# Gate and up products of a conv FFN: from three 256-column products to one of 512 and one of 256, with each exit split over steps

## The chip, the core and the metric

The kernel runs on one core of one Trainium2 chip. Engines with queues of their own work side by side: PE (TensorE) does matrix products and, as PEld, loads their stationary operands; DVE (VectorE) and ACT (ScalarE) do elementwise work; SP issues most of the DMA loads and POOL a few. Each engine takes its instructions strictly in the order in which the program issued them, and an instruction that has to wait holds up all behind it on its engine. The metric is the device time of one execution in microseconds (us); the median of three runs of the kernel before is 438.47 us.

## What is computed

One layer of a small hybrid block over 256 tokens with 1024 channels: a token mixer (block attention and retention), a layer norm, a convolutional feed-forward part, a layer norm. The change touches the feed-forward part alone:

```python
def conv_ffn(h, w_ff_gate, w_ff_up, ff_conv_w, ff_conv_b, w_ff_down):
    s = h.shape[1]
    g = h @ w_ff_gate
    u = h @ w_ff_up
    gp = jnp.pad(g, ((0, 0), (CONV_WIDTH - 1, 0), (0, 0)))
    g_conv = sum(gp[:, j:j + s, :] * ff_conv_w[j] for j in range(CONV_WIDTH)) + ff_conv_b
    a = jax.nn.gelu(g_conv, approximate=False) * u
    return a @ w_ff_down
```

D_FF is 2816, the convolution is three tokens wide, and all is in float32.

## The kernel before

**Precision.** A float32 value is held as two tiles, high and low: high is the value copied into PE's float32r type, low is what is left. `split` (line 64) makes them: ACT copies the high part, DVE subtracts. A product of two such values is three products on PE (`mm3`, line 79): high × high (line 80), high × low (81) and low × high (82).

**Units and steps.** The weights come from memory in units of 128 × 2048 (1 MB), each used in two halves of 1024 columns. From line 230 on, the program is a list of steps; a step uses one half (or, at the two groups by `weights4`, several). The main loop (line 1055) goes through the steps in order. In step s it first runs the side work (`run_sides`, generators such as `residual`, which multiplies and adds the first norm's rows, line 966), then prepares halves ahead (`prep_to`, `prep_halves`): ACT writes `whi` (line 1009) and DVE `wlo` (line 1023), and the raw buffer that comes free is filled by the next load on SP's queue (`load_raw`, line 73, 4 buffers). At most 8 prepared halves are alive; in the FFN the kernel prepares one more in each step, whose buffers are those that the step before has given back. Then it issues the step's products and, at the end of a unit, its exit. Some weight units of the modulation vector run through the same stream and are reduced on DVE (`ada`, line 147).

**The FFN.** A unit r of 256 hidden channels has a gate product (`ffn_gate`), an up product (`ffn_up`) and a down product (`mk_down`); there are NR = 11. The tokens' hidden state after the first norm, transposed, lies in four tiles: `S["h2h"]` (high, slots 3a and 3b) and `S["h2l"]` (low, slots 6a and 6b), each 128 × 4 × 256. In `wstat8` (line 287) a gate or up half is 128 hidden channels by 256 tokens, summed over 8 k with 3 products of 256 columns each; both halves of a unit share one PSUM bank of 512 columns. Four banks (0 to 3) go round (`one_bank`).

Up units 0 and 1 are made in another form before the gates (`xs_group`, steps 52 to 55). From step 56 on the order is: gate 0, gate 1, gate 2, up 2, down 0, down 1, and then gate r, up r, down r − 1 up to r = 7; then gate and up of 8, 9 and 10; then the downs of units 7 to 10 in the order of the output (`tok0`, `tok1`), with the second norm. Each unit is two steps; gate 0 is steps 56 and 57, down 1 steps 66 and 67. Within gate 0, between its halves, PE transposes the last tokens of up 0 and 1 (`up_T`, line 577).

**The exits.** When both halves of a gate unit are done, `gate_done` (line 586) issues: ACT twice `Identity` with the convolution's middle weight and bias, out of PSUM (line 593); DVE four `scalar_tensor_tensor`, out of PSUM, for the other two taps (line 596); ACT `Gelu` (line 598). When an up unit is done, `act_in` (line 604) multiplies the up values in PSUM by the Gelu values on DVE (line 606) and splits the result into `ah` and `al` (lines 65 and 66), the stationary operands of `down` (line 615). For units 0 and 1 `act_in` follows the gate's exit at once. All of an exit is issued in one go, at the end of the unit's second step.

Of the kernel before, what the change touches and what calls it, by code (L numbers as in the profile page):

```python
# [7 lines left out]
F32 = mybir.dt.float32  # L8
# [42 lines left out]
def _body(nc, a, out, pe, act, dve, sp, cst, wts, big, tmp, ps, dram):  # L51
    f = lambda ap: ap.bitcast(F32)

    def bank(i):
        return ps.tile([128, 512], F32, tag=f"P{i}", name=f"P{i}")

    def slot(n, shape, dt=F32):
        return big.tile(shape, dt, tag=f"A{n}", name=f"A{n}")

    def halves(n):  # L60

        return [slot(n + e, [128, 4, 256], F32R) for e in "ab"]

    def split(hi, lo, src):
        act.activation(hi, src, AF.Copy)  # L65
        dve.tensor_tensor(lo, src, f(hi), OP.subtract)  # L66
# [12 lines left out]
    def mm3(o, lh, ll, rh, rl, start, stop):  # L79
        pe.matmul(o, lh, rh, start=start, stop=False)  # L80
        pe.matmul(o, lh, rl, start=False, stop=False)  # L81
        pe.matmul(o, ll, rh, start=False, stop=stop)  # L82

    def table(func):

        d_ = tmp.tile([128, 1], F32, name="dummy", bufs=1)
        act.activation(d_, epst, func)
# [13 lines left out]
    bcol = const("bcol", [128, 6, 8], nc.gpsimd)  # L101
    mod = cst.tile([128, 6, 8], F32, name="mod")

    raws = {}
    loads_A = [(dict(a="ada1", W="winA", X="winX")[n], j) for n, j in SEQ if n in "aWX"]

# [196 lines left out]
    def wstat4(name, u, xh, xl, done):  # L303
# [9 lines left out]
            return mm  # L313
        weights(a[name][u], mk(0), mk(1))

    S = {}
    ghh, ghl = (lambda k: hh[:, k]), (lambda k: hl[:, k])

# [200 lines left out]
        weights4(src, [mk(0, 0), mk(0, 1), mk(1, 0), mk(1, 1)], [range(4)] * 4)  # L519

    def out_start():
        S["h2h"], S["h2l"] = halves("3"), halves("6")
        GB = S["GB"] = tmp.tile([128, 2, 8], F32, name="GB", bufs=1)
        m = mod[:, 2:4]
        lncol = consts["lncol"]
        dve.tensor_tensor(GB[:, 0], lncol[:, 0], m[:, 0], OP.mult)
        dve.tensor_tensor(GB[:, 1], lncol[:, 1], m[:, 0], OP.mult)
        dve.tensor_tensor(GB[:, 1], GB[:, 1], m[:, 1], OP.add)
        table(AF.Sqrt)
# [46 lines left out]
    def up_T(t):  # L576
        p = bank(6 + t)
        for i in range(4):
# [4 lines left out]
             {(0, 1, "mid"): ln1_tok1, (0, 1): lambda p: up_tokens(0, p),  # L583
              (1, 1, "mid"): lambda: up_T(0), (1, 1): lambda p: (up_tokens(1, p), table(AF.Gelu))})

    def gate_done(r):
        def fn(p):
            g = slot(("5", "15")[r % 2], [128, 2, 256])
            pv = p.rearrange("p (i t) -> p i t", i=2)
            convw = consts["convw"]  # L590
            w = lambda n, i: convw[:, n, 2 * r + i:2 * r + i + 1]
            for i in range(2):
                act.activation(g[:, i], pv[:, i], AF.Identity, scale=w(2, i), bias=w(3, i))
            for n in (1, 0):
                for i in range(2):
                    dve.scalar_tensor_tensor(g[:, i, 2 - n:], pv[:, i, :254 + n], w(n, i), g[:, i, 2 - n:],
                                             op0=OP.mult, op1=OP.add)
            act.activation(g, g, AF.Gelu)
            S["gelu", r] = g
            if r < 2:  # L600
                act_in(r, S["uT"][:, 2 * r:2 * r + 2].rearrange("p a b -> p (a b)"))
        return fn

    def act_in(r, u):
        g = S.pop(("gelu", r)).rearrange("p a b -> p (a b)")
        dve.tensor_tensor(g, u, g, OP.mult)
        ah = slot(("9a", "9b", "10a", "8a")[r % 4], [128, 2, 256], F32R)
        al = slot(("2a", "2b", "4", 0)[r % 4], [128, 2, 256], F32R)
        split(ah.rearrange("p a b -> p (a b)"), al.rearrange("p a b -> p (a b)"), g)
        S["a", r] = ah, al  # L610

    def up_done(r):
        return lambda p: act_in(r, p)

    def down(r, t, hf, hl_, cs, first, last, p=None):
        ah, al = S["a", r]
# [34 lines left out]
    def tok0(i):  # L651
        def fn(ts):
            if i == 0:
                table(AF.Sqrt)
            for hf in range(2):
                down(NR - NG + i, 0, hf, ts[hf], BOTH, False, i == NG - 1 and hf == 1)
            if i == NG - 1:
                n = Norm(S["x1"][:, 0], S["g", 1], S["z2"][0], ("6a", "6b"))
                for c, w in BOTH:
                    n.piece(c, w, S["yf"][c // 512])  # L660
                S["rows"] = out_rows(n, 0, BOTH)
                next(S["rows"])
        return fn
# [23 lines left out]
                    pass  # L687
        return fn

    def ffn_gate(r):  # L690
        wstat8("wgate", r, gh2, gl2, gate_done(r))

    def ffn_up(r):
        wstat8("wup", r - 2, gh2, gl2, up_done(r))

    def first():
        bank_i[0] = 0
        up_T(1)

    wstat8("wgate", 0, gh2, gl2, gate_done(0), first)  # L700
    ffn_gate(1)
    for r in range(2, NR):
        ffn_gate(r)
# [169 lines left out]
    def retention():  # L873
        rT, decay, sms = S["rT"], S["decay"], S["sms"]
        while S["main"] < RV_AT:
            yield
            yield
            yield
        rv = S["rv"]
        yr = [slot(n, [128, 1024]) for n in ("8a", "8b")]  # L880
        stt = tmp.tile([128, 8, 6], F32, name="stt", bufs=1)
        mv = tmp.tile([128, 8, 2], F32, name="mvr", bufs=1)
        sd = tmp.tile([128, 8], F32, name="sdr", bufs=1)
        ds_ = {}
        for h in range(HR + 2):
            yield
            if h > 1:
                g = h - 2
                for t in range(2):
                    dve.bn_stats(stt[:, 2 * g + t], yr[t][:, g * 256:(g + 1) * 256])  # L890
                    dve.bn_aggr(mv[:, 2 * g + t], stt[:, 2 * g + t:2 * g + t + 1])
            yield
            if 0 < h <= HR:
                g = h - 1
                d_ = ds_.pop(g)
                p = bank(7)
                c = slice(g * 256, (g + 1) * 256)
                pe.matmul(p[:, 0:256], d_[:, 0:128], rv[0][:, c], start=True, stop=True)
                pe.matmul(p[:, 256:512], d_[:, 128:256], rv[0][:, c], start=True, stop=False)
                pe.matmul(p[:, 256:512], d_[:, 256:384], rv[1][:, c], start=False, stop=True)  # L900
                for t in range(2):
                    act.activation(yr[t][:, c], p[:, t * 256:(t + 1) * 256], AF.Copy)
            if h < HR:
                p = bank(4)
                pe.matmul(p[:, 0:256], rT[1][:, h, 0:128], rT[0][:, h, :], start=True, stop=True)
                pe.matmul(p[:, 256:384], rT[1][:, h, 128:256], rT[0][:, h, 128:256], start=True, stop=True)
                d_ = sms[:, (HM + h) % (TL + 2)]
                dve.tensor_tensor(d_, p[:, :384], decay[h // 2][:, h % 2], OP.mult)
                ds_[h] = d_
            yield  # L910
        S["x"] = [slot(n, [128, 1024]) for n in ("2a", "2b")]
        for i in range(2):
            nc.gpsimd.dma_start(S["x"][i], a["x"][i])
        yield
        act.activation(sd, mv[:, :, 1], AF.Sqrt, bias=epst)
        dve.reciprocal(sd, sd)
        yield
        yield
        while S["main"] < RG_AT:
            yield  # L920
            yield
            yield
        srg = S["rg"]
        for g in range(HR + 1):
            yield
            if g:
                for t in range(2):
                    act.activation(yr[t][:, c], yr[t][:, c], AF.Copy, scale=sd[:, 2 * g + t - 2:2 * g + t - 1])
            if g < HR:
                c = slice(g * 256, (g + 1) * 256)  # L930
                for t in range(2):
                    dve.scalar_tensor_tensor(yr[t][:, c], yr[t][:, c], mv[:, 2 * g + t, 0:1], srg[t][:, c],
                                             op0=OP.subtract, op1=OP.mult)
            yield
            yield
        yrh, yrl = halves("3"), halves("6")
        S["yrh"], S["yrl"] = yrh, yrl
        for _ in range(3):
            yield
        for w in range(2):  # L940
            for t in range(2):
                yield
                yield
                p = bank(4 + t)
                for i in range(4):
                    pe.transpose(p[:, i * 128:(i + 1) * 128],
                                 yr[t][:, w * 512 + i * 128:w * 512 + (i + 1) * 128], ident)
                pv = p.rearrange("p (i t) -> p i t", i=4)
                split(yrh[w][:, :, t * 128:(t + 1) * 128], yrl[w][:, :, t * 128:(t + 1) * 128], pv)
                yield  # L950
# [99 lines left out]
    def run_sides():  # L1050
        for g in list(sides):
            if next(g, StopIteration) is StopIteration:
                sides.remove(g)

    for s, (need, rel, fn) in enumerate(steps):
# [6 lines left out]
        if not late:  # L1062
            prep_to(max(need) + 1 + (LOOKAHEAD if s < LN1_AT - 1 else HL_BUFS))
        run_sides()
        fn([tiles[h] for h in need])
        for h in rel:
            tiles.pop(h)
# [100 lines left out]
```

## Time and profile before

| what | value |
|---|---|
| median of three runs | 438.47 us (438.03 to 438.67) |
| the profiled execution, device time | 439.22 us |
| its span, first to last instruction | 437.4 us |
| PE, DVE, ACT busy | 420.7, 345.9, 241.4 us |
| FFN in the trace | gate 0 from 253.8 us, last up ends at about 407, last product ends at about 429.9 |
| units in it | 11 gates, 9 ups, 11 downs |
| mean granted clock | 0.994 |

The page gives the busy time of each engine and its share of the span; the chain of waits follows the work that ended last back to its start. A row of the timeline has the start in us from the span's beginning, the duration, engine, line, operation, result and operands, shape and count; what stands in brackets is the idle time before it and what ended it. A row with a count over one shows several instructions in sequence as one piece. A matmul's duration includes its passage through the array, so that the distance from start to start is what it costs in a stream.

### The profile page before, as it was taken

Reading aid. Unit: us, or ns where it says so; the run is one execution under the profiler, and the core shown is the slowest. Engines: PE = TensorE matmul, PEld = TensorE weight load, DVE = VectorE, ACT = ScalarE, POOL = GpSimd, SP = SyncE. Lnnn points to the kernel's source line nnn. Section 1 sums busy time; section 2 is a strip of 40 time slices with the busy share of each in tenths; the row PEclk is TensorE's granted clock in tenths of the full one; section 3 lists DMA queues with packets and bytes.
Section 4 is the critical chain, followed back from the end, with each engine's and each line's share of the span. In section 5 each row is a group of like instructions: output and inputs, shape, how many; then the busy total and the mean of one; then the engine's idle time right before and its main releaser. Section 6 shows DMA issues by size and latency. Waiting matters only on the chain.

```text
span 437.4 us, 6902 instructions
## 1 busy us (share of the span) xinstructions
PE 420.7 (96%) x2732; PEld 379.7 (87%) x2732; DVE 345.9 (79%) x547; ACT 241.4 (55%) x368; POOL 7.3 (2%) x17
## 2 busy tenths in 40 slices
PE   2999999999999999999999999999999999999993
PEld 1878888777788999999989899899999999999882
DVE  4888689969997999698779887798896665576476
ACT  4366568579873469543443894665445445355500
POOL 0000000000000000000000010000000000000000
PEclk9999999999999999999999999999999999999997
DMA  7998997795468778789664069477766774550001
GB/s 266 397 417 338 335 339 281 291 349 211 180 239 306 285 288 303 267 289 352 222 240 145 0 232 412 166 273 272 283 227 254 290 263 171 194 192 2 1 24 72
DMA packets 19728, 105.72 MB, mean 242 GB/s; under 512 B 2528, under 2 KB 4592, under 8 KB 8432
## 3 DMA queue, kind: packets, MB, share of 16 engines
q1 hardware_dynamic: 18288, 100.27, 61.5%
q0 software_dynamic: 1408, 5.01, 3.3%
q8 instruction: 21, 0.34, 0.3%
q14 instruction: 11, 0.09, 0.0%
HBM read 104.22 MB, written 1.06 MB: 241 GB/s over the span
## 4 chain that ended last, share of the span: by engine, by line
PE 83%; DVE 9%; ACT 3%; DMA 2%; issue 1%; SPq 1%; DVEq 0%; ACTq 0%
PE P L80 25%; PE P L82 25%; PE P L81 25%; DVE junk L147 3%; DMA raw<-in_ada 2%; DVE wlo L1023 2%; ACT whi L65 1%; DVE wlo L66 1%; PE P L513 1%; PE P L516 1%; PE P L515 1%; PE P L809 1%; PE P L828 1%; PE P L852 1%; SPq L73 1%
## 5 line engine op out<-in xcount | busy, mean ns | idle before, releaser
L1023 DVE TENSOR_TENSOR wlo<-raw,whi 128x1024 fp32r<-128x1024 f32 x118 | 140.6, 1220 | 24.7 <-ACT whi L1009 24.7
L1009 ACT ACTIVATE whi<-raw 128x1024 fp32r<-128x1024 f32 x118 | 120.2, 1052 | 41.0 <-PE P L82 11.9
L82 PE MATMUL P<-whi,A 128*128 128x512 f32 (+1 forms) x228 | 87.3, 383 | 0.0
L80 PE MATMUL P<-whi,A 128*128 128x512 f32 (+1 forms) x184 | 72.9, 396 | 5.4 <-ACT A L65 5.3
L81 PE MATMUL P<-wlo,A 128*128 128x512 f32 (+1 forms) x184 | 71.0, 386 | 0.0
L147 DVE CUSTOM_DVE_ANT_0 junk<-raw,srow 128x1024 bf16<-128x1024 f32 (+1 forms) x49 | 58.8, 1200 | 1.5 <-DMA raw<-in_ada 1.1
L80 PE MATMUL P<-A3a,whi 128*128 128x256 f32 x192 | 54.4, 283 | 0.0
L82 PE MATMUL P<-A3b,wlo 128*128 128x256 f32 x192 | 54.4, 283 | 0.0
L81 PE MATMUL P<-A6a,whi 128*128 128x256 f32 x192 | 54.4, 283 | 0.0
L80 PE MATMUL P<-A3b,whi 128*128 128x256 f32 x192 | 54.4, 283 | 0.0
L81 PE MATMUL P<-A6b,whi 128*128 128x256 f32 x192 | 54.3, 283 | 0.0
L82 PE MATMUL P<-A3a,wlo 128*128 128x256 f32 x192 | 54.3, 283 | 0.0
L82 PEld LDWEIGHTS P<-whi,A 128*128 128x128 f32 x228 | 43.5, 191 | 8.8 <-DVE A L66 0.3
L80 PEld LDWEIGHTS P<-whi,A 128*128 128x128 f32 x184 | 35.3, 192 | 14.1 <-ACT A L65 6.6
L80 PE MATMUL P<-A,whi 128*128 128x256 f32 x160 | 46.0, 287 | 0.0
L81 PE MATMUL P<-A,whi 128*128 128x256 f32 x160 | 45.3, 283 | 0.0
L82 PE MATMUL P<-A,wlo 128*128 128x256 f32 x160 | 45.3, 283 | 0.0
L81 PEld LDWEIGHTS P<-wlo,A 128*128 128x128 f32 x184 | 35.2, 192 | 6.3
L80 PEld LDWEIGHTS P<-A3a,whi 128*128 128x128 f32 x192 | 36.8, 192 | 0.3
L81 PEld LDWEIGHTS P<-A6a,whi 128*128 128x128 f32 x192 | 36.8, 192 | 0.3
L81 PEld LDWEIGHTS P<-A6b,whi 128*128 128x128 f32 x192 | 36.9, 192 | 0.0
L80 PEld LDWEIGHTS P<-A3b,whi 128*128 128x128 f32 x192 | 36.9, 192 | 0.0
(227 smaller groups left out, 705.5 us busy)
## 6 DMA issues: line engine op xcount, KB each, us to landing
raw<-in_ada SPq DMA_DIRECT2D x23, 1024.0 KB, 5.7
raw<-in_wup SPq DMA_DIRECT2D x11, 1024.0 KB, 4.8
raw<-in_wgate SPq DMA_DIRECT2D x11, 1024.0 KB, 4.9
raw<-in_wdown SPq DMA_DIRECT2D x11, 1024.0 KB, 4.8
raw<-in_winB SPq DMA_DIRECT2D x10, 1024.0 KB, 6.8
raw<-in_winA SPq DMA_DIRECT2D x16, 256.0 KB, 6.9
raw<-in_winA SPq DMA_DIRECT2D x4, 1024.0 KB, 6.2
raw<-in_winGr SPq DMA_DIRECT2D x4, 1024.0 KB, 5.6
```

What stands on the lines that cost most here:

```text
L65: act.activation(hi, src, AF.Copy)
L66: dve.tensor_tensor(lo, src, f(hi), OP.subtract)
L73: sp.dma_start(t[:, i * n:(i + 1) * n], src[:, i * n:(i + 1) * n])
L80: pe.matmul(o, lh, rh, start=start, stop=False)
L81: pe.matmul(o, lh, rl, start=False, stop=False)
L82: pe.matmul(o, ll, rh, start=False, stop=stop)
L147: dve.tensor_tensor_reduce(out=junk[:, rows], in0=raw[:, rows], in1=srow[:, rows], scale=1.0, scalar=0.0, op0=OP.mult, op1=OP.add, accum_o ...
L513: pe.matmul(p, xl(k)[:, tk], hi[:, c], start=False, stop=k == 7)
L515: pe.matmul(p, xh(k)[:, tk], hi[:, c], start=k == 0, stop=False)
L516: pe.matmul(p, xh(k)[:, tk], lo[:, c], start=False, stop=False)
L1009: act.activation(hi, src, AF.Copy)
L1023: dve.tensor_tensor(lo, src, f(hi), OP.subtract)
```

## The change

The high and low parts of the hidden state are put beside each other in one tile, so that one product of 512 columns multiplies a weight tile with both; the product of the low weights with the high tokens stays 256 columns wide. Per k there are two products in place of three, with two weight loads in place of three. The bank now holds one half: columns 0 to 255 sum high × high and low × high, columns 256 to 511 high × low. Leaving the bank, ACT copies the second part into a tile, and DVE adds the first to it. Each half of a unit has a bank of its own, in a round of the same four.

The convolution's middle tap moves from ACT to DVE, and reads the tile instead of PSUM, as do the other two taps. The work of an exit is no longer issued in one go: `put_off` puts it on a list with the step at which it is due, and the main loop issues what is due after the preparation of halves and ahead of the step's products.

```diff
+    place = {"3a": ("Ya", 0), "6a": ("Ya", 1), "3b": ("Yb", 0), "6b": ("Yb", 1)}
+    pairs = {}
+
+    def reopen(dt, *names):
+        for n in names:
+            pairs[n] = big.tile([128, 2, 1024], dt, tag=f"A{n}", name=f"A{n}")
...
+    def mm2(o, wh, wl, x2, start, stop):
+        if start:
+            pe.matmul(o, wh, x2, start=True, stop=False)
+        pe.matmul(o[:, :256], wl, x2[:, 0], start=False, stop=False)
+        if not start:
+            pe.matmul(o, wh, x2, start=False, stop=stop)
...
+    def wstat8m(name, u, x2, copy, done, mid=None):
+        def mk(half):
+            def mm(hi, lo):
+                if half and mid:
+                    mid()
+                p = one_bank()
+                for k in range(8):
+                    mm2(p, hi[:, k * 128:(k + 1) * 128], lo[:, k * 128:(k + 1) * 128], x2(k), k == 0, k == 7)
+                t = copy(half)
+                act.activation(t, p[:, 256:], AF.Copy)
+
+                def rest():
+                    dve.tensor_tensor(t, p[:, :256], t, OP.add)
+                    done(half)
+                put_off(1, rest)
+            return mm
+        weights(a[name][u], mk(0), mk(1))
+
+    waiting = []
+
+    def put_off(n, fn):
+        waiting.append((S["main"] + n, fn))
...
     def out_start():
-        S["h2h"], S["h2l"] = halves("3"), halves("6")
+        S["h2"] = [slot("Y" + e, [128, 2, 4, 256], F32R) for e in "ab"]
+        S["h2h"], S["h2l"] = [[t[:, i] for t in S["h2"]] for i in range(2)]
...
     def gate_done(r):
-        def fn(p):
-            g = slot(("5", "15")[r % 2], [128, 2, 256])
-            pv = p.rearrange("p (i t) -> p i t", i=2)
+        def fn(half):
+            g, x = gu(r)[:, half], gu(r)[:, 2 + half]
             convw = consts["convw"]
-            w = lambda n, i: convw[:, n, 2 * r + i:2 * r + i + 1]
-            for i in range(2):
-                act.activation(g[:, i], pv[:, i], AF.Identity, scale=w(2, i), bias=w(3, i))
+            w = lambda n: convw[:, n, 2 * r + half:2 * r + half + 1]
+            dve.tensor_scalar(g, x, w(2), w(3), op0=OP.mult, op1=OP.add)
             for n in (1, 0):
-                for i in range(2):
-                    dve.scalar_tensor_tensor(g[:, i, 2 - n:], pv[:, i, :254 + n], w(n, i), g[:, i, 2 - n:],
-                                             op0=OP.mult, op1=OP.add)
-            act.activation(g, g, AF.Gelu)
-            S["gelu", r] = g
-            if r < 2:
-                act_in(r, S["uT"][:, 2 * r:2 * r + 2].rearrange("p a b -> p (a b)"))
+                dve.scalar_tensor_tensor(g[:, 2 - n:], x[:, :254 + n], w(n), g[:, 2 - n:],
+                                         op0=OP.mult, op1=OP.add)
+            if half:
+                put_off(min(r, 1), lambda: act.activation(gu(r)[:, :2], gu(r)[:, :2], AF.Gelu))
+                if r < 2:
+                    put_off(1 + r, lambda: act_in(r, S["uT"][:, 2 * r:2 * r + 2]))
         return fn
...
-        split(ah.rearrange("p a b -> p (a b)"), al.rearrange("p a b -> p (a b)"), g)
         S["a", r] = ah, al
+        put_off(min(r, 1), lambda: act.activation(ah, g, AF.Copy))
+        put_off(1 + min(r, 1), lambda: dve.tensor_tensor(al, g, f(ah), OP.subtract))
 
     def up_done(r):
-        return lambda p: act_in(r, p)
+        return lambda half: act_in(r, gu(r)[:, 2:]) if half else None
...
         run_sides()
+        for e in waiting:
+            if e[0] <= s:
+                e[1]()
+        waiting[:] = [e for e in waiting if e[0] > s]
         fn([tiles[h] for h in need])
```

`gu(r)` is a tile of 128 × 4 × 256 in slot 5 or 15: its first two parts hold the gate after the convolution, its last two what comes out of the banks (the gate's, then the up's). The slots 3a, 6a, 3b and 6b, which other stages use for other tiles, become views of the two paired tiles Ya and Yb; `reopen` makes these anew at three places (the start, the normalised retention output, the end).

More of the change, by code (lines that the diff above doesn't have):

```diff
@@ L55, in bank @@
         return ps.tile([128, 512], F32, tag=f"P{i}", name=f"P{i}")
-    def slot(n, shape, dt=F32):
-        return big.tile(shape, dt, tag=f"A{n}", name=f"A{n}")
+    place = {"3a": ("Ya", 0), "6a": ("Ya", 1), "3b": ("Yb", 0), "6b": ("Yb", 1)}
[3 more added lines that the diff above has]
+            pairs[n] = big.tile([128, 2, 1024], dt, tag=f"A{n}", name=f"A{n}")
+    def slot(n, shape, dt=F32):
+        if n not in place:
+            return big.tile(shape, dt, tag=f"A{n}", name=f"A{n}")
+        pair, e = place[n]
+        assert pairs[pair].dtype == dt
+        v = pairs[pair][:, e, :math.prod(shape[1:])]
+        return v.rearrange("p (a b) -> p a b", a=shape[1]) if len(shape) == 3 else v
     def halves(n):
@@ L102, in _body @@
     mod = cst.tile([128, 6, 8], F32, name="mod")
+    reopen(F32, "Ya", "Yb")
     raws = {}
@@ L584, in _body, with gu @@
               (1, 1, "mid"): lambda: up_T(0), (1, 1): lambda p: (up_tokens(1, p), table(AF.Gelu))})
+    def gu(r):
+        if ("gu", r) not in S:
+            S["gu", r] = slot(("5", "15")[r % 2], [128, 4, 256])
+        return S["gu", r]
     def gate_done(r):
-        def fn(p):
-            g = slot(("5", "15")[r % 2], [128, 2, 256])
-            pv = p.rearrange("p (i t) -> p i t", i=2)
+        def fn(half):
+            g, x = gu(r)[:, half], gu(r)[:, 2 + half]
             convw = consts["convw"]
-            w = lambda n, i: convw[:, n, 2 * r + i:2 * r + i + 1]
-            for i in range(2):
-                act.activation(g[:, i], pv[:, i], AF.Identity, scale=w(2, i), bias=w(3, i))
+            w = lambda n: convw[:, n, 2 * r + half:2 * r + half + 1]
+            dve.tensor_scalar(g, x, w(2), w(3), op0=OP.mult, op1=OP.add)
             for n in (1, 0):
-                for i in range(2):
-                    dve.scalar_tensor_tensor(g[:, i, 2 - n:], pv[:, i, :254 + n], w(n, i), g[:, i, 2 - n:],
-                                             op0=OP.mult, op1=OP.add)
-            act.activation(g, g, AF.Gelu)
-            S["gelu", r] = g
-            if r < 2:
-                act_in(r, S["uT"][:, 2 * r:2 * r + 2].rearrange("p a b -> p (a b)"))
+                dve.scalar_tensor_tensor(g[:, 2 - n:], x[:, :254 + n], w(n), g[:, 2 - n:],
[4 more added lines that the diff above has]
+                    put_off(1 + r, lambda: act_in(r, S["uT"][:, 2 * r:2 * r + 2]))
         return fn
     def act_in(r, u):
-        g = S.pop(("gelu", r)).rearrange("p a b -> p (a b)")
+        g = gu(r)[:, :2]
         dve.tensor_tensor(g, u, g, OP.mult)
@@ L657, in fn @@
             if i == NG - 1:
+                reopen(F32, "Ya", "Yb")
                 n = Norm(S["x1"][:, 0], S["g", 1], S["z2"][0], ("6a", "6b"))
@@ L688, in tok1, with ffn_gate @@
         return fn
-    def ffn_gate(r):
-        wstat8("wgate", r, gh2, gl2, gate_done(r))
+    h2 = lambda k: S["h2"][k // 4][:, :, k % 4]
+    def ffn_gate(r, mid=None):
+        wstat8m("wgate", r, h2, lambda half: gu(r)[:, 2 + half], gate_done(r), mid)
     def ffn_up(r):
-        wstat8("wup", r - 2, gh2, gl2, up_done(r))
+        wstat8m("wup", r - 2, h2, lambda half: gu(r)[:, 2 + half], up_done(r))
     def first():
-        bank_i[0] = 0
         up_T(1)
-    wstat8("wgate", 0, gh2, gl2, gate_done(0), first)
+    ffn_gate(0, first)
     ffn_gate(1)
@@ L935, in retention @@
             yield
+        reopen(F32R, "Ya", "Yb")
         yrh, yrl = halves("3"), halves("6")
```

## The prediction

> **What bounds the kernel now.** I read the page first (shares, then the chain of waits), then busy times by stretch, then the timeline of each engine in the FFN.
>
> ```profile
> span 437.4 us, 6902 instructions
> PE 420.7 (96%) x2732; PEld 379.7 (87%) x2732; DVE 345.9 (79%) x547; ACT 241.4 (55%) x368; POOL 7.3 (2%) x17
> PE 83%; DVE 9%; ACT 3%; DMA 2%; issue 1%; SPq 1%; DVEq 0%; ACTq 0%
> 257.00:280.00 23.00, 23.00 (x183) 22.53 (x182) 17.95 (x25) 14.80 (x22) 2.08 (x4) 1.00 0.85 328
> 280.00:300.00 20.00, 20.00 (x135) 18.55 (x134) 17.46 (x23) 11.43 (x14) 0.00 (x0) 1.00 0.72 257
> 300.00:320.00 20.00, 20.00 (x135) 18.52 (x134) 16.43 (x23) 9.63 (x12) 0.00 (x0) 1.00 0.66 252
> 340.00:360.00 20.00, 20.00 (x147) 19.04 (x147) 13.24 (x18) 9.53 (x12) 1.07 (x2) 1.00 0.78 289
> ```
>
> The columns after the stretch are its length and the busy time of PE, PEld, DVE, ACT and POOL. In the FFN, PE is never idle, at full clock; it sets the end. But DVE is at 87% from 280 to 300, so it has little to spare where the change gives it work.
>
> How PE spends its time is read from start to start of its products:
>
> ```profile
> 282.05 0.39 PE L80 MATMUL P<-whi,A9a 128*128 128x512 f32 x1
> ...
> 283.87 0.39 PE L82 MATMUL P<-whi,A2b 128*128 128x512 f32 x1
> ...
> 299.32 0.28 PE L80 MATMUL P<-A3b,whi 128*128 128x256 f32 x1
> 299.44 0.28 PE L81 MATMUL P<-A6b,whi 128*128 128x256 f32 x1
> 299.56 0.28 PE L82 MATMUL P<-A3b,wlo 128*128 128x256 f32 x1
> 299.68 0.40 PE L80 MATMUL P<-whi,A10a 128*128 128x512 f32 x1
> ...
> 304.93 0.39 PE L82 MATMUL P<-whi,A 128*128 128x512 f32 x1
> 305.15 0.28 PE L80 MATMUL P<-A3a,whi 128*128 128x256 f32 x1
> ```
>
> After a 256-column product the next starts 0.120 us later, whatever its width. The eight starts of 512 columns from 282.05 to 283.87 are 0.2275 us apart, less than two of 256; the one before a 256 (304.93 to 305.15) is no longer.
>
> **What PE gains.** Each k of a gate or up half now takes three products of 256 columns (0.360 us), and then one of 512 and one of 256 (0.2275 + 0.120): 0.0125 us less. There are 20 units (11 gate, 9 up) of 2 halves and 8 k: 320 × 0.0125 = 4.0 us, 0.10 us for each half. The moving operand of the new product comes in two runs of 256 columns; no row shows such an operand. Its price lies between nothing and 0.0125 us (which would make 512 columns as dear as two 256s, and the gain nil); I take nothing, since all the rows of 512, whose operands are weight tiles, are alike.
>
> The Trainium skill (TensorE: Matmul & The Clock Gate, section Back-to-back issue gap) gives a warm gap of N / 2.4 plus about 2.5 ns, so that merging two products saves only the 2.5 ns: an estimate of 320 × 2.5 ns = 0.8 us. The rows show 12.5 ns where the page has 2.5, and the measurement decides.
>
> **What the exits cost.** Before, a gate unit leaves PSUM after both halves: two L593 on ACT, four L596 on DVE, Gelu. After, each half leaves with a copy of 256 columns on ACT, then on DVE an add (out of PSUM), a tensor_scalar, and two scalar_tensor_tensor, each on the result of the one before. An up half gets a copy and an add. The rows for these, DVE first (the line of L470 is a group: count, busy us, mean ns):
>
> ```profile
> 238.22 0.67 DVE L449 TENSOR_SCALAR A<-A,mv,sd 128x768 f32<-128x768 f32 x1
> L470 DVE TENSOR_SCALAR A7b<-P,GB 128x128 f32<-128x128 f32 x8 | 2.7, 404 | 0.5 <-PE P L457 0.5
> 257.33 5.77 DVE L1023 TENSOR_TENSOR wlo<-raw,whi 128x1024 fp32r<-128x1024 f32 x5 [1.53 <-ACT whi L1009]
> 263.01 1.65 DVE L596 SCALAR_TENSOR_TENSOR A<-P,convw,A 128x255 f32<-128x255 f32 x4
> 265.42 0.69 DVE L606 TENSOR_TENSOR A<-A,A 128x512 f32<-128x512 f32 x1 [0.76 <-ACT A L598]
> 287.37 0.69 DVE L966 TENSOR_TENSOR A<-A,A 128x512 f32<-128x512 f32 x1
> 287.97 2.35 DVE L1023 TENSOR_TENSOR wlo<-raw,whi 128x1024 fp32r<-128x1024 f32 x2
> 429.92 0.42 DVE L402 TENSOR_TENSOR A6a<-P,AR 128x256 f32<-128x256 f32 x1 [0.51 <-PE P L82]
> 430.38 0.42 DVE L403 TENSOR_TENSOR A7b<-A7b,A6a 128x256 f32<-128x256 f32 x1
> 141.32 0.38 ACT L902 ACTIVATE A8a<-P 128x256 f32<-128x256 f32 x1 [3.10 <-PE P L900]
> 141.60 0.38 ACT L902 ACTIVATE A8b<-P 128x256 f32<-128x256 f32 x1
> 256.25 4.84 ACT L1009 ACTIVATE whi<-raw 128x1024 fp32r<-128x1024 f32 x5
> 264.76 0.63 ACT L598 ACTIVATE A<-A 128x512 f32<-128x512 f32 x1 [2.28 <-DVE A L596]
> 266.15 0.63 ACT L65 ACTIVATE A9a<-A 128x512 fp32r<-128x512 f32 x1 [0.76 <-DVE A L606]
> 266.69 1.99 ACT L1009 ACTIVATE whi<-raw 128x1024 fp32r<-128x1024 f32 x2
> ```
>
> A dependent step costs its duration and 0.03 (430.38 − 429.92 = 0.46 after a 0.42); an independent one starts about 0.08 before the other ends, so a wlo holds DVE 1.14 (five in 5.77) and a 512-column step 0.60 (287.97 − 287.37). A scalar_tensor_tensor is 0.48, or 0.39 with independent neighbours. The tensor_scalar isn't shown at this size: by proportion of L449 0.22, on the line through L470 (0.40 for 128) and L449 (0.67 for 768) 0.46. I take 0.41, nearer to the upper row, as the small size pays mostly a fixed part. A gate half then holds DVE 0.46 + 0.44 + 0.51 + 0.39 = 1.80 us, a unit 3.6 where it was 1.6; an up unit gets two adds, 0.8 more. The ACT copy is 0.38, holds 0.28, and is no dearer than what it replaces in a gate.
>
> **Where that lands: the first ten steps of the FFN.** Main steps 56 to 66 are gate 0, gate 1, gate 2, up 2 (two halves each), down 0 (64, 65) and the first half of down 1 (66). That half's third product reads al of unit 1, which L66 wrote well ahead before (the row is below). In the changed program al(1) is issued in step 64, and DVE works strictly in order. Ahead of it, from 257.33, stand: wlo of halves 60 to 71 (one more is issued in each step, ahead of that step's deferred work), 12 × 1.14 = 13.7; six gate halves (gates 0, 1, 2), 6 × 1.80 = 10.8; the multiplication and al of unit 0 and the multiplication of unit 1, 3 × 0.60 = 1.8; the add of the first up half, 0.35. Together 26.6. DVE also stands still where ACT's queue makes it wait: ACT holds gelu(0), behind which come a copy and whi(66), which the next wlo needs, so that after the exit of gate 0 DVE idles 0.1 + 0.55 + 0.28 + 1.05 = 2.0; behind ah(0) 0.3; behind gelu(2) 0.6. That is 257.33 + 26.6 + 2.9 = 286.8, and al(1), at 0.69, ends at 287.5.
>
> ```profile
> 273.83 0.69 DVE L66 TENSOR_TENSOR A2b<-A,A9b 128x512 fp32r<-128x512 f32 x1 [0.70 <-ACT A9b L65]
> ...
> 282.73 0.39 PE L80 MATMUL P<-whi,A9b 128*128 128x512 f32 x1
> 282.96 0.39 PE L81 MATMUL P<-wlo,A9b 128*128 128x512 f32 x1
> 283.19 0.39 PE L82 MATMUL P<-whi,A2b 128*128 128x512 f32 x1
> ```
>
> A2b is al(1): it was written by 274.5, and its reader started at 283.19. With eight halves 0.10 faster PE would be there at 282.4. It waits until 287.5: **5.1 us** of stops. Some 2 us fall earlier, because a gate or up half now takes a bank of four: up 2's halves need banks 0 and 1 back from gate 1, whose adds come out of the same DVE queue about 1 us late each. The other 3 us fall at step 66.
>
> Bounds: all six tensor_scalars at 0.22 take 1.1 off; 0.1 more on every new step adds 2.5 (24 in the gates, one add). So stops of 4.0 to 7.6, and with the 4.0 gained a net of 0 to +3.6; my value is **+1.1**.
>
> **After that** nothing else waits. A cycle of gate, up and down takes PE 16.6 us, and DVE gets 2 + 0.8 = 2.8 more in it: from 280 to 300 17.46 + 2.8 × 20 / 16.6 = 20.8 of 20, from 300 to 320 19.8, then less. A lag of 1 us is covered: wlo is prepared eight halves ahead, and a bank is asked for again five steps (14 us) after its product while downs stand between, three steps (8 us) in the last gates, where DVE (13.24 of 20 now) has room. If that cover were gone, this lag would be paid, 1 to 2 us. The loads on SP's queue follow wlo as before, 4 buffers ahead. The paired h2 tile holds the same bytes in the same order of writes, so everything ahead of step 56 costs nothing more: writers and readers stay far apart under PE's products. The tail from 418 on has the same steps; al(10) is wanted in the fourth tail step, 8 us after its copy, and needs about 4.
>
> **The clock** adds to this. What a stop of PE does to it shows only at the ends of the run:
>
> ```profile
> 10.33 0.80 PE L80 MATMUL P<-whi,A 128*128 128x512 f32 x1 [5.26 <-ACT A L65]
> 12.20 0.63 PE L81 MATMUL P<-wlo,A 128*128 128x512 f32 x1
> 12.63 0.63 PE L82 MATMUL P<-whi,A 128*128 128x512 f32 x1
> 15.61 0.40 PE L80 MATMUL P<-whi,A 128*128 128x512 f32 x1
> 431.00:432.00 1.00, 0.00 (x0) 0.00 (x0) 0.93 (x3) 0.29 (x1) 0.00 (x0) 1.00 0.00 0
> 432.00:433.00 1.00, 0.00 (x0) 0.00 (x0) 1.00 (x4) 0.00 (x0) 0.00 (x0) 0.51 0.00 0
> ```
>
> The last product ended by 429.92 (L402 above waited for it), and from 432.0 on the granted clock is one half: 2.1 us of rest were enough. At the start, after a wait of 5.26 us, products of 512 columns start 0.43 us apart (12.20, 12.63) until 15.6: the 5.3 us from 10.33 on at this pace cost 5.3 × (1 − 0.23 / 0.43) = 2.5 us. A stop of 3 us in step 66 may bring this: 0 to 2.5, and I take 0.9, since one sighting at an end says little of when the clock falls within.
>
> The Trainium skill (same page, section What's actually happening) has the clock halved after an idle window of about 3.4 us, and back after a busy one. An estimate by it: 3.4 × 0.47 = 1.6 us if the stop fills enough of a window. The trace's fall after 2.1 us of rest is earlier than a whole window.
>
> **Sum.** 437.4 − 4.0 + 5.1 + 0.9 = 439.4 us of span, +2.0. The profiled execution lasted 439.22 (1.8 around its span), 0.75 over the median 438.47; on the scale of the median, **440.5 us**.
>
> **Rivals.** (1) The stops happen, but the clock holds: +1.1, 439.6; for it, the stop is in pieces; against it, the fall after 2.1 us. (2) The start of the FFN is covered: al(1) and the banks come in time because DVE gets through the first exits faster than I add them up, the place being steps 60 to 66. Net is zero at al(1) by 286.4, and faster by over 0.2% from 285.5 down; fully covered (by 282.4) the time is 438.47 − 4.0 = 434.5. Against it: the twelve wlo alone end no earlier than 271.0, and the rest are rows. For it: PE now waits nowhere, and the margin there was large. Midway, 436.5. (3) The two-run operand costs the 0.012: no gain, DVE's queue unchanged, so 287.5 − 283.2 = +4.3: 442.8. (4) DVE lags through 280 to 330 as well and the banks come late there too: 1 to 2 us on top, 442.0.
>
> **How the numbers follow.** Stops with some loss of clock 0.42 (439.7 to 442), stops with the clock held 0.30 (437.8 to 440.2), start covered 0.16 (434.5 to 437.6), no gain 0.05, lag throughout 0.07. A run of this kernel can tell 0.2%, 0.9 us, from no change. Faster takes most of the covered case, 0.14. The held clock lies across the border of 439.35: its lower half is no change, with the edges of its neighbours 0.22. Slower has the rest, 0.64. The range leaves out the covered case and the worst: 437.0 to 442.2.
>
> **What would show it.** Right: products of 512 and 256 in the gates at 0.227 and 0.120; PE idle between about 271 and 288 with DVE's add and L66's successor (al) as releasers, 5 us in sum, and none later; the fall of the clock visible in the stretch after it. Wrong: PE without idle time in that stretch, or a spacing that isn't 0.23 for the new product, or waits of PE for DVE after 300.

## The result, and the profile after

The changed kernel takes 440.8 us (median of 10 runs, 439.22 to 441.35), the kernel before 438.17 us (median of 10): ratio 1.0054, 95% interval 1.0038 to 1.0069. The change makes it slower by 0.4 to 0.7%; 440.5 us was predicted.

The page of the changed kernel, and its busy times by stretch (length, then PE, PEld, DVE, ACT, POOL, then the granted clock):

```profile
span 439.4 us, 6373 instructions
PE 418.8 (95%) x2412; PEld 363.5 (83%) x2412; DVE 371.6 (85%) x609; ACT 244.2 (56%) x386; POOL 7.3 (2%) x17
257.00:280.00 23.00, 21.41 (x118) 18.14 (x117) 20.45 (x32) 12.71 (x21) 1.72 (x4) 1.00 0.81 314
280.00:300.00 20.00, 17.30 (x80) 14.14 (x79) 18.00 (x28) 10.15 (x14) 0.00 (x0) 0.91 0.62 214
300.00:320.00 20.00, 20.00 (x109) 17.22 (x108) 19.68 (x31) 10.01 (x15) 0.00 (x0) 1.00 0.72 262
340.00:360.00 20.00, 20.00 (x106) 17.08 (x105) 17.34 (x27) 10.49 (x15) 1.08 (x2) 1.00 0.78 270
```

PE has 320 products fewer and is busy 1.9 us less, but between 257 and 300 it now has gaps, and in the second of these stretches its clock was not full. DVE got 25.7 us more work; from 300 to 320 it is busy 19.68 of 20 us, and still PE does not wait there.

Where PE stops is seen in its timeline. The rows are product starts; what stands in brackets is the idle time before and its releaser:

```profile
269.68 0.40 PE L105 MATMUL P<-AYb,whi 128*128 128x512 f32 x1
270.95 0.47 PE L102 MATMUL P<-AYa,whi 128*128 128x512 f32 x1 [0.86 <-DVE A L354]
...
273.57 0.39 PE L105 MATMUL P<-AYb,whi 128*128 128x512 f32 x1
274.69 0.47 PE L102 MATMUL P<-AYa,whi 128*128 128x512 f32 x1 [0.73 <-DVE A L354]
...
283.25 0.39 PE L95 MATMUL P<-wlo,A9b 128*128 128x512 f32 x1
286.34 0.80 PE L96 MATMUL P<-whi,A2b 128*128 128x512 f32 x1 [2.71 <-DVE A2b L665]
286.94 0.63 PE L94 MATMUL P<-whi,A9b 128*128 128x512 f32 x1
287.36 0.63 PE L95 MATMUL P<-wlo,A9b 128*128 128x512 f32 x1
...
289.07 0.59 PE L96 MATMUL P<-whi,A2b 128*128 128x512 f32 x1
289.50 0.40 PE L94 MATMUL P<-whi,A9b 128*128 128x512 f32 x1
```

The two halves of up 2 wait for the add (L354) that frees their bank, and the third product of down 1 waits for al of unit 1 (A2b, written by L665). Over the 0.23 us of a product these are stops of 1.04, 0.89 and 2.86 us, 4.8 in all. Behind the third one the next product starts 0.60 us later and the others 0.42 to 0.43 apart until 289.5: seven in 3.16 us (286.34 to 289.50), where 7 × 0.2275 = 1.59 would do. That is 1.57 us, called lost clock below; some 0.1 of it belongs to the first product, which takes longer behind a wait at full clock too (0.33 us in e8 below).

What the queue of DVE did in the meantime: the first wlo, the exit of the first gate half, the longest wait, and al(1):

```profile
256.17 5.77 DVE L1081 TENSOR_TENSOR wlo<-raw,whi 128x1024 fp32r<-128x1024 f32 x5 [1.53 <-ACT whi L1067]
261.86 0.42 DVE L354 TENSOR_TENSOR A<-P,A 128x256 f32<-128x256 f32 x1
262.31 0.41 DVE L648 TENSOR_SCALAR A<-A,convw 128x256 f32<-128x256 f32 x1
262.76 1.00 DVE L650 SCALAR_TENSOR_TENSOR A<-A,convw 128x255 f32<-128x255 f32 x2
263.68 1.22 DVE L1081 TENSOR_TENSOR wlo<-raw,whi 128x1024 fp32r<-128x1024 f32 x1
...
268.64 1.23 DVE L1081 TENSOR_TENSOR wlo<-raw,whi 128x1024 fp32r<-128x1024 f32 x1 [1.92 <-ACT whi L1067]
...
282.46 1.22 DVE L1081 TENSOR_TENSOR wlo<-raw,whi 128x1024 fp32r<-128x1024 f32 x1
283.60 0.41 DVE L354 TENSOR_TENSOR A<-P,A 128x256 f32<-128x256 f32 x1
284.46 1.22 DVE L1081 TENSOR_TENSOR wlo<-raw,whi 128x1024 fp32r<-128x1024 f32 x1 [0.45 <-ACT whi L1067]
285.61 0.68 DVE L665 TENSOR_TENSOR A2b<-A,A9b 128x512 fp32r<-128x512 f32 x1
```

A gate half holds DVE from 261.86 to 263.68, 1.82 us. al(1) starts 29.4 us after the first wlo (285.61 − 256.17), and of these DVE stood still for 2.4, waiting for ACT's whi (1.92 and 0.45).

The gain is read from a stretch without downs, here by the first product of a gate or up half:

```profile
387.25 0.39 PE L102 MATMUL P<-AYa,whi 128*128 128x512 f32 x1
...
406.85 0.40 PE L102 MATMUL P<-AYa,whi 128*128 128x512 f32 x1
```

Seven halves lie between: 2.80 us each, where one took 24 × 0.120 = 2.88. So a half gains 0.08 us and all 40 gain 3.2.

The sum over the FFN, from the first product of gate 0 to the last product of all: before 253.82 to 429.60, 175.79 us; after 252.66 to 431.58, 178.93. It is longer by 3.14 us, and −3.2 + 4.8 + 1.57 = +3.2. The two spans differ by 2.0 only because the FFN began 1.2 us earlier in the second profile.

By the times, the lost clock isn't in every execution; the one with a profile (441.2 us) shows it. The ten times fall in two groups: six from 440.76 to 441.35, with a mean granted clock of 0.992 or 0.993, and four from 439.22 to 439.87, with 0.997. The groups are 1.5 us apart.

### The profile page after: what moved, and what is told of

Read it like the earlier page. It is cut to its first block, busy times and chain, and to the rows that moved or that the text cites. A ratio compares the mean times of both kernels' runs of the same rounds, so it can differ in the third digit from the quotient of the medians.

```text
span 439.4 us, 6373 instructions
## 1 busy us (share of the span) xinstructions
PE 418.8 (95%) x2412; PEld 363.5 (83%) x2412; DVE 371.6 (85%) x609; ACT 244.2 (56%) x386; POOL 7.3 (2%) x17
## 3 DMA queue, kind: packets, MB, share of 16 engines
HBM read 104.22 MB, written 1.06 MB: 240 GB/s over the span
## 4 chain that ended last, share of the span: by engine, by line
PE 92%; DVE 4%; ACT 1%; DMA 1%; issue 1%; DVEq 0%; POOLq 0%
PE P L94 20%; PE P L96 20%; PE P L95 20%; PE P L105 14%; PE P L103 8%; PE P L102 2%; DMA bcol<-in_bcol 1%; DVE wlo L1081 1%; PE P L563 1%; PE P L565 1%; PE P L566 1%; PE P L814 1%; PE P L866 1%; PE P L885 1%; PE P L909 1%
## 5 line engine op out<-in xcount | busy, mean ns | idle before, releaser
L1067 ACT ACTIVATE whi<-raw 128x1024 fp32r<-128x1024 f32 x118 | 122.5, 1054 | 39.5 <-PE P L96 14.5
L105 PE MATMUL P<-AYb,whi 128*128 128x512 f32 x160 | 57.7, 396 | 0.0
L103 PE MATMUL P<-AYb,wlo 128*128 128x256 f32 x160 | 44.6, 279 | 0.0
L105 PE MATMUL P<-AYa,whi 128*128 128x512 f32 x120 | 44.0, 396 | 0.0
L103 PE MATMUL P<-AYa,wlo 128*128 128x256 f32 x160 | 38.1, 279 | 0.0
L351 ACT ACTIVATE A<-P 128x256 f32<-128x256 f32 x40 | 15.3, 381 | 39.5 <-PE P L105 36.3
L105 PEld LDWEIGHTS P<-AYb,whi 128*128 128x128 f32 x160 | 30.0, 188 | 7.2
L103 PEld LDWEIGHTS P<-AYa,wlo 128*128 128x128 f32 x160 | 30.2, 188 | 3.4
L80 DVE TENSOR_TENSOR wlo<-raw,whi 128x1024 fp32r<-128x1024 f32 (+1 forms) x22 | 24.4, 1126 | 8.9 <-ACT whi L79 8.8
L94 PEld LDWEIGHTS P<-A,whi 128*128 128x128 f32 x160 | 30.6, 192 | 0.4 <-issue 0.4
L95 PEld LDWEIGHTS P<-A,whi 128*128 128x128 f32 x160 | 30.7, 192 | 0.0
```

The lines of the kernel that those rows point to most:

```text
L103: pe.matmul(o[:, :256], wl, x2[:, 0], start=False, stop=False)
L105: pe.matmul(o, wh, x2, start=False, stop=stop)
L351: act.activation(t, p[:, 256:], AF.Copy)
```

## The experiments

Theory: at the start of the FFN, DVE's queue is behind, the exits and al(1) come out of it late, PE stops for 4.8 us in the first ten steps and loses clock in the longest stop, and this outweighs what the products gain. The rivals are the round of banks alone, DVE's sum of work whatever its order, and the new products. Length is that from gate 0's first product to the last of all in the profiled execution; the kernel before has 175.79 in both of its profiles.

| kernel | median us | ratio to before | length us |
|---|---|---|---|
| changed | 440.8 | 1.0054 (1.0038 to 1.0069) | 178.93 |
| e1, down 1 later | 436.7 | 0.9967 (0.9955 to 0.9979) | 174.46 |
| e2, unit 1 sooner | 437.03 | 0.9972 (0.9962 to 0.9982) | 174.70 |
| e3, nothing put off | 447.76 | 1.0212 (1.0192 to 1.0231) | 185.61 |
| e5, exits first | 434.6 | 0.9924 (0.9910 to 0.9938) | 172.79 |
| e6, gates 0 and 1 old | 434.88 | 0.9923 (0.9911 to 0.9936) | 172.64 |
| e8, filled stop | 439.29 | 1.0031 (1.0019 to 1.0043) | 177.48 |
| e9, e6 with one run | 435.05 | 0.9930 (0.9918 to 0.9943) | 172.64 |
| e10, e6 with wide first | 436.12 | 0.9953 (0.9940 to 0.9966) | 173.97 |

**e1, down 1 later.**

```diff
-        if r < NR - NG + 1:
+        if r == 3:
+            weights(a["wdown"][1], mk_down(1, 0), mk_down(1, 1))
+        if 2 < r < NR - NG + 1:
             weights(a["wdown"][r - 1], mk_down(r - 1, 0), mk_down(r - 1, 1))
```

> The changed kernel with one edit: down 1 stands two units later in the order (behind gate 3 and up 3, ahead of down 2), so that al of unit 1 is wanted 11 us later. Theory (DVE's queue at the start of the FFN is late with al(1), and the clock falls in that stop): the stop of 2.9 us at down 1 and the stretch at half clock are gone, the two stops of about 1 us at up 2 stay; against the kernel before 1.9 - 3.2 = -1.3 us, ratio 0.997. Rival (the bank round is what costs; al(1) would only have covered it): the stops move to gate 3 and the time stays at 1.005. Rival (the new products themselves are slower than they look): no fall below 1.003.

The two stops of up 2 are in its trace at the same places, 1.04 and 0.85 us by the starts:

```profile
271.03 0.47 PE L102 MATMUL P<-AYa,whi 128*128 128x512 f32 x1 [0.87 <-DVE A L354]
274.77 0.47 PE L102 MATMUL P<-AYa,whi 128*128 128x512 f32 x1 [0.68 <-DVE A L354]
```

The length falls to 174.46, 1.33 less than before: −3.2 and these two. Neither the stop of 2.9 us nor a stretch at half clock is left, and no stop came at gate 3. One edit that takes nothing off any engine turns the change into a gain; the round of banks alone is not the cause, and the new products are not slow.

**e2, unit 1 sooner.**

```diff
-                put_off(min(r, 1), lambda: act.activation(gu(r)[:, :2], gu(r)[:, :2], AF.Gelu))
+                put_off(int(r > 1), lambda: act.activation(gu(r)[:, :2], gu(r)[:, :2], AF.Gelu))
...
-                    put_off(1 + r, lambda: act_in(r, S["uT"][:, 2 * r:2 * r + 2]))
+                    put_off(1, lambda: act_in(r, S["uT"][:, 2 * r:2 * r + 2]))
...
-        put_off(min(r, 1), lambda: act.activation(ah, g, AF.Copy))
-        put_off(1 + min(r, 1), lambda: dve.tensor_tensor(al, g, f(ah), OP.subtract))
+        put_off(int(r > 1), lambda: act.activation(ah, g, AF.Copy))
+        put_off(1 + int(r > 1), lambda: dve.tensor_tensor(al, g, f(ah), OP.subtract))
```

> The changed kernel with one edit: Gelu, multiplication, ah and al of units 0 and 1 are put off by one step less or two (unit 1 as unit 0 is), the order of units is as in the changed kernel. Theory: al(1) is then issued in step 62 instead of 64, so that it stands ahead of two wlo (2.3 us) and an add in DVE's queue; the stop at down 1 shrinks from 2.9 to about 0.4 us, the two at up 2 stay, the clock holds; against the kernel before -0.9 us, ratio 0.998. Rival (what is late is DVE's sum of work, wherever al(1) stands): the stop at down 1 keeps over 1.5 us, ratio above 1.001.

From the timeline of DVE in this kernel:

```profile
281.66 1.23 DVE L1081 TENSOR_TENSOR wlo<-raw,whi 128x1024 fp32r<-128x1024 f32 x1
282.80 0.69 DVE L665 TENSOR_TENSOR A2b<-A,A9b 128x512 fp32r<-128x512 f32 x1
283.40 0.42 DVE L354 TENSOR_TENSOR A<-P,A 128x256 f32<-128x256 f32 x1
```

al(1) starts at 282.80 instead of 285.61, and the length is 174.70. PE's rest in front of its reader shrinks to 0.1 us over a product (starts 0.334 apart), the stops of up 2 are as before the edit. The same work in another place of the queue ends 2.8 us sooner, so the sum of DVE's work is not what makes al(1) late.

**e3, nothing put off.**

```diff
     def put_off(n, fn):
-        waiting.append((S["main"] + n, fn))
+        fn()
```

> The changed kernel with one edit: what is put off is issued at once, so that the copy, the add, the convolution, Gelu and the split of a half stand in the queues right behind its products, ahead of the next wlo. Theory: the order in the queues decides. At the start of the FFN the exits then stand ahead of the wlo that nobody needs yet, and the stops at up 2 shrink to about 0.1 us each, with none at down 1; but all through the FFN DVE waits in turn for ACT's copy, Gelu and ah, and with about 0.9 of its time taken it falls behind for good: stops of PE at banks after 320, 445 to 448 us. Rival (putting off by a step is what makes the start late, and costs nothing elsewhere): 435 to 436 us and no stop after 300.

At the start it is as the theory has it: one stop of 0.3 us at up 2 and none at down 1. But the length is 185.61, and the time 447.76. The waits of this kernel from 250 us on (who waited for whom: total, times, longest):

```profile
ACT A L653 <- DVE A L650: 63.1, 11, 8.1
...
PE P L102 <- DVE A L354: 6.6, 6, 1.6
PE P L94 <- ACT A10a L664: 1.8, 1, 1.8
```

ACT stands at Gelu for 63.1 us (13.1 in the changed kernel), with the copy and whi of later halves behind it, and PE stops at banks again and again. The last row, a stop of 1.8 us at 422.33, was followed by 3.4 us at half clock (see the last section). Putting off by a step is worth far more than it costs; what was too long were its distances at the start (e2), and what stood ahead of it within a step (e5, below).

**e5, exits first.**

```diff
         run_sides()
+        for e in waiting:
+            if e[0] <= s:
+                e[1]()
+        waiting[:] = [e for e in waiting if e[0] > s]
         prep_to(max(need) + 1, True)
...
         run_sides()
-        for e in waiting:
-            if e[0] <= s:
-                e[1]()
-        waiting[:] = [e for e in waiting if e[0] > s]
         fn([tiles[h] for h in need])
```

and the edits of e2.

> The changed kernel with two edits: what is due in a step is issued ahead of that step's preparation of a half instead of behind it, and units 0 and 1 are put off by the lesser number of steps of the second experiment. Theory: what stood in front of the banks' adds and of al(1) was wlo that PE needs 20 us later; with the exits in front, stops of 0.1 us at most are left at up 2 and none at down 1, and all 40 halves keep their 0.08: -3.1 us against the kernel before, ratio 0.993. Rival (DVE's sum of work is what is late, and the order only moves it): about -1 us as with the second experiment.

One stop of 0.3 us is left, at up 2, where 0.1 at most was expected. This is faster than both kernels: 434.6 us, and all 40 halves are in the new form. The stretches:

```profile
257.00:280.00 23.00, 22.86 (x124) 19.46 (x123) 19.17 (x31) 11.54 (x19) 1.06 (x3) 1.00 0.78 287
280.00:300.00 20.00, 20.00 (x104) 17.05 (x103) 19.06 (x29) 10.53 (x16) 0.00 (x0) 1.00 0.62 226
```

DVE does as much as in the changed kernel (38.23 us of these 43, 38.45 there), and PE is held for 0.3 us alone.

**e6, gates 0 and 1 in the old form.**

```diff
...
-    ffn_gate(0, first)
-    ffn_gate(1)
+    wstat8("wgate", 0, gh2, gl2, gate_old(0), first)
+    wstat8("wgate", 1, gh2, gl2, gate_old(1))
```

`gate_old` is the exit of the kernel before, with the split behind it, writing into the tiles of `gu`.

> Gates 0 and 1 in the form of the kernel before (three products of 256 columns, one exit for the unit, issued at once), all other units in the new form. Theory: in the 22 us in which DVE is behind it has 2 x 2.0 us less to do and the banks of gates 0 and 1 aren't asked for again soon; no stop of PE is left, the clock holds, and 36 halves gain 0.08 us each: -2.9 us against the kernel before, ratio 0.9935. Rival (the stops come from the new exit as such and move to gates 2 to 4): stops of 1 us or more after 280, ratio 0.997 to 1.003.

```profile
257.00:280.00 23.00, 23.00 (x145) 20.75 (x144) 19.35 (x29) 13.70 (x21) 1.06 (x3) 1.00 0.82 301
280.00:300.00 20.00, 20.00 (x104) 17.05 (x104) 19.30 (x29) 10.74 (x15) 0.00 (x0) 1.00 0.77 272
```

PE has no gap in the FFN at all. The length is 3.15 us less than before, 36 × 0.08 = 2.9 expected; the time, 434.88, agrees. The new exit as such stops nothing once the start is over.

**e8, the stop filled.**

```diff
     def mk_down(r, half):
         def mm(hi, lo):
+            if r == 1 and half == 0:
+                p = bank(2)
+                for i in range(12):
+                    pe.matmul(p, S["a", 0][0][:, 0, :128], hi[:, :512], start=i == 0, stop=i == 11)
```

The products are extra work that nothing reads.

> The changed kernel with 12 products of 512 columns that nothing reads, put ahead of down 1 into a bank that is free by then: 2.7 us of work of PE that fill the stop there. Theory (the clock falls in some executions because PE rests for 2.9 us): no execution has the stretch at half clock; the times lose their upper group (440.8 to 441.4) and all lie in the lower (439.2 to 439.9), ratio 1.003. Rival (the two groups have another cause): two groups as before, or the lower one 2.7 us longer.

The timeline of PE:

```profile
283.20 2.88 PE L684 MATMUL P<-whi,A9a 128*128 128x512 f32 x12
285.92 0.39 PE L94 MATMUL P<-whi,A9b 128*128 128x512 f32 x1
286.15 0.39 PE L95 MATMUL P<-wlo,A9b 128*128 128x512 f32 x1
286.55 0.50 PE L96 MATMUL P<-whi,A2b 128*128 128x512 f32 x1
286.88 0.40 PE L94 MATMUL P<-whi,A9b 128*128 128x512 f32 x1
```

The reader of al(1) starts no sooner, 286.55, but the products behind it run at full clock. The length is 1.45 us less than that of the changed kernel, with 2.7 us more work in it. The upper group is gone: seven runs, 438.92 to 440.21. So the 1.5 us between the groups are the clock lost through PE's rest; that the four runs of the lower group kept their clock follows from the times, no profile shows one.

**e9 and e10, the spacing of the new products,** both on e6. e9 lays high and low parts of each k side by side, e10 puts the 512 ahead of the 256 for every k.

```diff
-        S["h2"] = [slot("Y" + e, [128, 2, 4, 256], F32R) for e in "ab"]
-        S["h2h"], S["h2l"] = [[t[:, i] for t in S["h2"]] for i in range(2)]
+        S["h2"] = [slot("Y" + e, [128, 4, 2, 256], F32R) for e in "ab"]
+        S["h2h"], S["h2l"] = [[t[:, :, i] for t in S["h2"]] for i in range(2)]
...
-    h2 = lambda k: S["h2"][k // 4][:, :, k % 4]
+    h2 = lambda k: S["h2"][k // 4][:, k % 4]
```

```diff
-        if start:
-            pe.matmul(o, wh, x2, start=True, stop=False)
-        pe.matmul(o[:, :256], wl, x2[:, 0], start=False, stop=False)
-        if not start:
-            pe.matmul(o, wh, x2, start=False, stop=stop)
+        pe.matmul(o, wh, x2, start=start, stop=False)
+        pe.matmul(o[:, :256], wl, x2[:, 0], start=False, stop=stop)
```

> The kernel with gates 0 and 1 in the old form, and one more edit: high and low parts lie side by side for each k (128 x 4 x 2 x 256), so that the moving operand of the 512-column product is one run of 512 and not two of 256. In the changed kernel a 512 and a 256 take 0.234 + 0.116 = 0.350 us from start to start, where the rows of before have 0.2275 + 0.120 = 0.3475. Theory A (the second run costs the 2.5 ns): 0.2275 + 0.120, and 36 x 8 x 2.5 ns = 0.7 us off the kernel without this edit (434.9): 434.2. Theory B (the price lies elsewhere): 0.350 as before, no change within 0.3 us.

> The kernel with gates 0 and 1 in the old form, and one more edit: for every k the 512-column product comes first and the 256-column one behind it (in the changed kernel so only for the first k). If the extra 2.5 ns of a pair come from the 512 columns being summed into a bank region that the 256 before has just written, they stay the same, since the order in the stream is the same but for the first k; one fewer pair of two 256s in sequence in each half: no change within 0.3 us of 434.9. Rival (the order of the two matters for the loading of the weights): spacing other than 0.350 a pair.

e9's length is that of e6 to the hundredth: the two runs of the operand cost nothing, and the extra 2.5 ns lie elsewhere. e10 was expected to change nothing, and is 1.33 us longer. Its timeline shows 1.06 us for three pairs:

```profile
395.71 0.40 PE L101 MATMUL P<-AYa,whi 128*128 128x512 f32 x1
395.95 0.28 PE L102 MATMUL P<-AYa,wlo 128*128 128x256 f32 x1
396.06 0.40 PE L101 MATMUL P<-AYa,whi 128*128 128x512 f32 x1
...
396.77 0.40 PE L101 MATMUL P<-AYa,whi 128*128 128x512 f32 x1
```

That is 0.353 a pair, and about 1.0 of the 1.33 us lies in the gate and up halves; the rest stands in the products of the downs. Why the order matters, the runs don't tell.

**e11, the kernel before once more.**

> The kernel before, unchanged, for a second profile. In the first one its FFN starts 1.1 us later (253.8) than the changed kernel's (252.8), though the code ahead of it does the same work. Theory: this is the scatter of the load at the very start from execution to execution; a second profile has a span of 436 to 437.5, mostly with the FFN's start moved and the same length from there to the end. Rival: the paired tiles have made the front of the changed kernel faster by 1 us; then the start stays at 253.8.

Its span is 436.5, its FFN starts at 252.85 and is as long as in the first profile (175.79). The changed kernel's starts at 252.66, and those of the other runs with paired tiles between 251.95 and 252.83. The first profile lost its time between the 201st and the 401st product of PE, which take 43.3 us in it, 42.4 in the second and 42.35 in the changed kernel. So 1.0 of the 1.2 us ahead of the FFN is scatter from execution to execution; that the paired tiles gain a few tenths there is not excluded.

## Why the prediction was right

- **The products.** 4.0 us were counted, 3.2 came. The step that was mis-sized is the pair of 512 and 256, taken as 0.2275 + 0.120 = 0.3475 from rows that don't alternate; alternating they take 0.234 and 0.116, together 0.350 (2.80 us for 8 pairs), 20% of the gain. The bound on the other side, that an operand in two runs might eat it all, is refuted by this, and by e9 none of the 2.5 ns comes from the two runs.
- **The exit of a half** was put at 1.80 us of DVE; it holds it for 1.82. The tensor_scalar, guessed at 0.41 between 0.22 and 0.46, takes 0.41.
- **The queue.** al(1) was to start 29.5 us after the first of the five wlo (286.8 − 257.33); it starts 29.4 us after it. That this agrees to 0.1 is luck in part, since two errors of half a microsecond cancel: DVE stood still for 2.4 us, not 2.9, and the work ahead of al(1) took 27.1, not 26.6. DVE's wait that follows Gelu of unit 0 was put at 2.0, and is 1.92. The three stops were placed at the two halves of up 2 and at the third product of down 1, at about 1, 1 and 3 us, 5.1 in all; they are 1.04, 0.89 and 2.86. e1, e2 and e5 show that the place in the queue is the cause.
- **Nothing later.** DVE is busy 19.68 of 20 us from 300 to 320 (19.8 was worked out), and the trace has no wait of PE for it after 300. From 280 to 300, where 20.8 of 20 was worked out, it is busy 18.00, in a stretch in which PE, with its long stop, worked 17.30.
- **The clock** was given 0.9 us between 0 and 2.5; it costs 1.57 where it falls, in six of ten runs, 0.9 as a mean. The median has it, which is why rival (1), stops with the clock held and priced at 439.6, came out for the other four runs alone. Which group has the median was luck: with two of the six runs in the other one it would lie below 440.
- **The total.** The net over the FFN was to be +2.0 and is +3.1 in the profiled execution: 0.8 of this is the smaller gain, 0.7 the clock, and the stops took 0.3 off. That the span, 439.4, is the one predicted is in part luck, since this execution reached the FFN 1.2 us earlier than the one the sum was made from. The ratio's interval, +0.38 to +0.69%, holds 440.5 / 438.47 = +0.46%. Rival (2), the start of the FFN covered, was priced at 4.0 us less than before; e5, where it is covered but for 0.3 us, takes 3.5 less (434.6, where the kernel before took 438.09 beside it), by the smaller gain of the products.

By the Trainium skill's formula for the isolated gap of one product (TensorE: Matmul & The Clock Gate, section Back-to-back issue gap) a merged pair would save 2.5 ns, an estimate; the traces show 10 (0.360 − 0.350). On the clock, the same page of the Trainium skill, section What's actually happening, is borne out in one part: the stretch at half clock has the length of its window (about 3.4 us; here a mean clock of 0.57 over the 4 us from 286 on is 3.4 us at one half, and the products are slow until 289.50). But PE had rested from 283.6 on, less than such a window, when the clock fell soon after 286.

## What to carry to other kernels

A busy share of 80% or so says how much work an engine can take on over a stretch, not what a strict queue does at the stretch's start: count what stands ahead of the instruction that is wanted, in the order of issue. Prepared work that is needed 20 us later (eight halves of 2.8 us here) should not stand ahead of an exit that frees a bank or feeds the next product; here the order of issue alone decided between +0.5% (the changed kernel) and −0.8% (e5). When a change adds work to an engine that is nearly full, look whether the first few units can keep the old form.

## What the runs showed of the hardware

The granted clock fell after about 2.5 us of rest in the middle of the kernel (PE's product of 283.25 ended by 283.64, and the clock is full until 286 and then not):

```profile
283.00:286.00 3.00, 0.64 (x3) 0.19 (x1) 2.55 (x4) 2.37 (x4) 0.00 (x0) 1.00 0.43 183
286.00:290.00 4.00, 3.66 (x10) 2.90 (x11) 3.97 (x6) 1.58 (x2) 0.00 (x0) 0.57 0.74 262
```

In e3 a shorter rest did it. PE rested for 1.77 us there, up to 422.33, and the clock was one half from 424 to 427.4:

```profile
420.50:424.00 3.50, 1.73 (x7) 1.11 (x7) 2.51 (x5) 2.34 (x3) 0.00 (x0) 0.99 0.00 0
424.00:427.40 3.40, 3.40 (x10) 2.38 (x9) 2.02 (x4) 0.73 (x2) 0.00 (x0) 0.51 0.00 0
```

Three rests of 1.5 to 1.6 us earlier in the same kernel (ahead of 344.88, 393.36 and 406.41) left it full. How long a rest must be for the fall isn't settled by these runs: in the changed kernel, by the times, it came in six executions of ten, so that a stop of 3 us costs either 3 or 4.5. Twelve products that nothing reads, in that rest, made the kernel 1.5 us faster. And the order of the two products of a pair, with the same weight loads and the same columns, moves a pair from 0.350 to 0.353 us; with what it adds in the downs, that is 1.3 us over the kernel.
